# Trainium2 study: a closer-spaced SSD scan, earlier z loads, norm sums on VectorE and pooling weights split in the mixing stage of a hybrid decoder step

## The chip, the cores and the metric

One Trainium2 chip, one core. The kernel is one launch that computes the whole layer. The metric is device time in microseconds (us), the median of repeated executions. The profile is one further execution, taken with the hardware profiler. Engines: PE (TensorE matmul, with PEld for its weight loads), DVE (VectorE), ACT (ScalarE), POOL (GpSimd), SP (SyncE, which here issues nearly all transfers, from one queue in program order).

## What is computed

One layer on 1024 prompt tokens and 8 x 8 sample tokens, model width 1024, all in fp32. Cut to its frame:

```python
x = x + 0.5 * swiglu(rmsnorm(x, norm_ffn1), ffn1_w_in, ffn1_w_out)
mix = token_mixing(rmsnorm(x, norm_mix), ...)
x = x + mix
x = x + 0.5 * swiglu(rmsnorm(x, norm_ffn2), ffn2_w_in, ffn2_w_out)
# token_mixing:
u, z, xbc, dt_raw, gate_logits = split(hn @ w_in)
branch_pool = pool_mix(u_ext, ...) @ pool_w_out
xs, bm, cm = causal_conv(xbc)
y = ssd_scan(xs, dt, A, bm, cm, h0) + d_skip * xs
yg = y * silu(z)                       # then an RMS norm in 4 groups of 512 channels
branch_ssd = (norm(yg) * ssd_norm) @ ssd_w_out
mix = (gates[0] * branch_pool + gates[1] * branch_ssd) @ w_o
```

`ssd_scan` is the chunked Mamba-2 recurrence: chunks of 128 tokens, 32 heads in 4 groups. Each of the 8 sample sequences carries its own state of 32 x 64 x 128 numbers, which is read, updated and written back.

## The kernel before, in words

The tokens are held transposed (channels on partitions) in two halves: half 0 has 512 prompt tokens, half 1 has 512 prompt tokens and the 64 sample tokens (576 columns). Each fp32 product is made of three matmuls on split operands: high by high, low by high, high by low. Weights arrive as fp32 (`wraw`), ACT rounds them to a high part `wh` and DVE subtracts to get the low part `wl`. Weights that are used twice can be split once and kept in DRAM as two arrays ("parted"); `load_w` then loads the two parts, 512 KB in place of 256 KB, and no split is needed.

The stages, in order of time: FFN 1 (input product in a Winograd-like form, names `pw`; output product `po`), the mixing's input projection, the mixing itself, FFN 2. Beside FFN 1 a side chain, `part`, splits weights for later: it loads a block (`pr`), splits it, stores both parts (`part<-ph`, `part<-pr`), and goes on to the next. Before, it goes over 12 blocks of `ffn1_w_out`, 12 of `ffn2_w_in`, 16 of `w_o` and 16 of `pool_w_out`. At the end of the input product the kernel finishes what is left of it (`finish(side)`), before the hidden rows (`hr`, `hp`) are loaded for the output product.

The mixing stage runs, on PE: `pool_branch` for both halves (`pgm`, then `pbp` with `pool_w_out`), then for each half four products with `ssd_w_out` (`pso`, one for each group g of 512 channels; the fourth is inside `merge`), then `out_proj` with `w_o` (`pwo`). I call these the dense products. The input of the product of group g is the scan of that group: `ssd_group` goes over 4 chunks (5 in half 1, the fifth being the samples). Each chunk is a step `ssd_a` (load the decay rows `ab`, transposes `pxT`, products `pcb`, many DVE and ACT operations on `ab`), a state update `ssd_st` (`pst`, `hst`), and `ssd_b` (`pyo`, `pyd`). For samples `ssd_b` runs over 8 units, each of which loads 256 KB of state `h`, transposes it (`ph0T`), updates it on DVE (`pnew`, L1375) and stores it. After a group's last chunk `gating` multiplies the scan's output `xs` by `z`, sums squares (`sq`, `ssq`), sends the sum through PE (`pss`), takes the inverse root on POOL (`rsm`), scales, and splits the result into `yhl`, the input of `pso`.

What sets the order: scan, gating and side work are Python generators. Each yields a delay, counted in PE work issued so far (`pe[0]`); `tick()`, called between the dense products, steps the generator that is due first. `STEP` is the delay between the steps of a scan for each half, `STEP_S` that between the sample units, `GP` that in gating, `PART_PACE` that of the side chain. When a dense product needs a group that is not gated, `scanned()` steps the scan to its end at once, with nothing dense in between. A scheduler then lays out each engine's instructions and assigns buffers: 42 buffers `act` serve all these tiles, 3 hold `xs` of whole groups, and `gating` may be at most two groups ahead of the products (`freed`).

Of the kernel before, what the change touches and what calls it, by code (L numbers as in the profile page):

```python
# [12 lines left out]
ALU = mybir.AluOpType  # L13

P = 128
D = 1024
KD = D // P
# [13 lines left out]
NTOK = (512, 576)  # L31
# [9 lines left out]

PRODUCTS = (("1", 0), ("2", 1), ("6", 0), ("5", 2), ("7", 0), ("3", 2), ("4", 0))

STEP = (7.0, 7.0)
STEP_S = 2.5
POST = 1.0
GP = (0.7, 1.2)
HN_AT, HN_PACE = 25.0, 2.0
MP = 2.0
R_WAIT0 = 2.0  # L50
# [3 lines left out]
T_AT, T_PACE = 2.0, 1.5  # L54
TURN_AT, CONST_AT = 60.0, 40.0
HP, HP_ST = 40, 0
PART_AT, PART_W, PART_PACE = 20.0, 4.0, 2.5


@with_exitstack  # L60
def tile_hybrid_pool_ssd_macaron(
# [303 lines left out]

        tr(out, r[:n, i : i + 1].broadcast_to([n, P]), ident[:n, :n])

    def rstd(tiles, h, count, out, pace=1.0, E=None):

        N = NTOK[h]  # L370
        nch = 4 + h
        s = act((P, N), name="ssq")
        for i, x in enumerate(tiles):
            if i == 0:
                S.activation(s, x, AF.Square)
            else:
                q = act((P, N), name="sq")
                S.activation(q, x, AF.Square)
                (E or V).tensor_tensor(s, s, q, op=ALU.add)  # L379
            if i % 2:  # L380
                yield pace
        yield max(pace, 1.5)
        pt = psum("ps", "pss")
        for c in range(nch):
            n = P if c < 4 else NS
            mm(pt[:n, c : c + 1], s[:, c * P : c * P + n], ones[:, 0:1])
        sm = small((P, 3, 5), "rsm", 2, pool=sp)
        v = sm[:, 2, :nch]
        if h == 1:
            G.memset(sm[:, 2, 4:5], 1.0)  # L390
        V.tensor_scalar(sm[:, 2, :4], pt[:, :4], 1.0 / count, EPS, op0=ALU.mult, op1=ALU.add)
        if h == 1:
            V.tensor_scalar(sm[:NS, 2, 4:5], pt[:NS, 4:5], 1.0 / count, EPS, op0=ALU.mult, op1=ALU.add)
        rsqrt(sm[:, 0, :nch], v)
        yield R_WAIT0
        r = act((P, N), name="r")
        pr = psum("ps", "prb")
        for c in range(4):
            along(pr[:, c * P : (c + 1) * P], sm[:, 0], c)
        S.copy(r[:, :512], pr)  # L400
        if h == 1:
            along(pt[:, 64:128], sm[:, 0], 4, NS)
            S.copy(r[:, 512:], pt[:, 64:128])
        yield R_WAIT
        out.append(r)
        yield 1.5
# [791 lines left out]
    def side():  # L1198
        yield from part(ffn1_w_out[0], out01)
        yield from part(ffn2_w_in[0], [(kb, 4, c0 + ff * P) for ff in range(N_PLAIN[0]) for kb in (0, 4) for c0 in (0, FF)])  # L1200
        for w in (w_o[0], pool_w_out[0]):
            yield from part(w, [(kb, 4, m * P) for m in range(KD) for kb in (0, 4)])

    ffn(wi1, ffn1_w_out[0], prep1, after1, side=side())
    ahead_d = in_proj(prep1m)
# [7 lines left out]
    def reload(h):  # L1213
# [4 lines left out]
            t.append(x_)  # L1218
        return t

    def pool_branch(h):

        N = NTOK[h]
        fh, fl = [None] * KD, [None] * KD
        d = {k: v for k, v in enumerate(ahead_d)} if h == 0 else {}

        def fetch_d(gi):
            for k in (2 * gi, 2 * gi + 1):
                if k not in d:
                    d[k] = load_d(h, k)  # L1230

        fetch_d(0)
        for gi in range(4):
            if gi < 3:
                fetch_d(gi + 1)
            dh, dl = zip(*(d.pop(k) for k in (2 * gi, 2 * gi + 1)))
            for j, pg in enumerate(dense2(wg[gi], 0, 0, [(h, dh, dl)], ("ps", "ps"), name="pgm")):
                m = gi * 2 + j
                fh[m], fl[m] = act((P, N), F32R, "fh"), act((P, N), F32R, "fl")
                for pt, (a, b) in zip(pg[0], PIECES[h]):  # L1240
                    split(pt[:, : b - a], fh[m][:, a:b], fl[m][:, a:b], cols[:, i_ps + m : i_ps + m + 1])
        for m in range(KD):
            t = act((P, N), name="t0")
            dma(t, gd[h][m])
            pb = dense(pool_w_out[0], 0, KD, m * P, [(h, fh, fl)], name="pbp")[0]
            for pt, (a, b) in zip(pb, PIECES[h]):
                V.scalar_tensor_tensor(t[:, a:b], t[:, a:b], 1.0, pt[:, : b - a], op0=ALU.add, op1=ALU.mult)
            dma(accd[h][m], t)

    def sample_parts(g, Bf, xs4, dtd3):  # L1250


        out = []
        for i in range(2):
            tok = slice(512 + 32 * i, 544 + 32 * i)
            xr = act((P, 5, 96), name="xr")
            S.copy(xr[:, :4, :].rearrange("p j (r t) -> p j r t", r=3), xs4[:, :, tok].unsqueeze(2).broadcast_to([P, 4, 3, 32]))
            S.copy(xr[:, 4, :].rearrange("p (r t) -> p r t", r=3), Bf[:, tok].unsqueeze(1).broadcast_to([P, 3, 32]))
            px, pb = psum("ps", "px3"), psum("ps", "pb3")
            for j in range(4):  # L1260
                tr(px[:96, j * P : (j + 1) * P], xr[:, j, :], ident)
            tr(pb[:96, :P], xr[:, 4, :], ident)
            xd, X3 = act((P, 512), name="xd3")[:96], act((P, 512), F32R, "X3")[:96]
            V.tensor_tensor(xd.rearrange("p (h d) -> p h d", d=HD), px[:96, :].rearrange("p (h d) -> p h d", d=HD),
                            dtd3[:, i, g * HPG : (g + 1) * HPG].unsqueeze(2).broadcast_to([96, HPG, HD]), op=ALU.mult)
            S.activation(X3, xd, AF.Copy)
            V.tensor_tensor(X3[32:64], xd[32:64], X3[32:64].bitcast(F32), op=ALU.subtract)
            B3 = small((96, P), "B3", 1, F32R)
            S.activation(B3, pb[:96, :P], AF.Copy)
            V.tensor_tensor(B3[64:96], pb[64:96, :P], B3[64:96].bitcast(F32), op=ALU.subtract)  # L1270
            bb = act((P, 4, P), F32R, "bblk")[:96]
            V.tensor_tensor(bb, B3.bitcast(F32).unsqueeze(1).broadcast_to([96, 4, P]),
                            bsel3.unsqueeze(2).broadcast_to([96, 4, P]), op=ALU.mult)
            out.append((X3, bb))
        return out

    def ssd_a(h, g, c, Bf, Cf, xs4, dts):
# [11 lines left out]
        for q in range(nq):  # L1289
            ab = act((P, hq, L), name="ab")  # L1290
            if smp:
                dma(ab, acs_sd[g * HPG : (g + 1) * HPG].partition_broadcast(P))
            else:
                r0 = g * HPG + q * hq
                dma(ab, acs_d[h][c, r0 : r0 + hq].partition_broadcast(P))
            abs_.append(ab)
        yield
        px = psum("ps", "pxT")
        for j in range(4):
# [12 lines left out]
        V.tensor_tensor(xp[:L, :].rearrange("p (h d) -> p h d", d=HD), px[:L, :].rearrange("p (h d) -> p h d", d=HD),  # L1312
                        dt[:L, hcs].unsqueeze(2).broadcast_to([L, HPG, HD]), op=ALU.mult)
        if smp:
            xd = sample_parts(g, Bf, xs4, cdp[1])
        else:
            xd = act((P, 512), name="xd")
            V.tensor_tensor(xd[:L, :].rearrange("p (h d) -> p h d", d=HD), px[:L, :].rearrange("p (h d) -> p h d", d=HD),
                            dtd[:L, hcs].unsqueeze(2).broadcast_to([L, HPG, HD]), op=ALU.mult)
# [14 lines left out]
    def ssd_b(h, g, c, a, hold, Cf, y4, dts):  # L1334
# [8 lines left out]
        if smp:  # L1343
# [16 lines left out]
                S.copy(hT.rearrange("p b n -> p (b n)"), pt)  # L1360
                return hT

            h0s = {0: load(units[0]), 1: load(units[1])}
            hTs = {}
            yield STEP_S
            for i, (pr, bh) in enumerate(units):
                if i + 2 < len(units):
                    h0s[i + 2] = load(units[i + 2])
                hTs[pr], h0 = turn(h0s[i]), h0s.pop(i)
                yield STEP_S  # L1370
                gp = g * 4 + pr
# [58 lines left out]
        hstate[g] = hn_  # L1430
        return hold

    def ssd_group(h, g, Bf, Cf, xs4, dts):
        y4 = xs4
        prev = None
        step = STEP[h]
        for c in range(4 + h):
            ga = ssd_a(h, g, c, Bf, Cf, xs4, dts)
            next(ga)
            yield step  # L1440
            try:
                next(ga)
            except StopIteration as e:
                a = e.value
            yield step
            if prev:
                for w in ssd_b(h, g, *prev, Cf, y4, dts):
                    yield w
            prev = (c, a, ssd_st(h, g, c, a, dts))
# [9 lines left out]
            dma(new_ssm_p[0, 0, g * HPG : (g + 1) * HPG].rearrange("(q h) p n -> (h p) q n", h=2),  # L1459
                fo.rearrange("p (q n) -> p q n", n=P))  # L1460

    def gating(h, g, y4, out):

        N = NTOK[h]
        E = V if (h, g) == (1, NG - 1) else G
        zs = []
        for j in range(4):
            z = act((P, N), name="z")
            dma(z, zd[h][g * 4 + j])
            zs.append(z)  # L1470
            if j % 2:
                yield GP[0]
        for j in range(4):
            E.tensor_tensor(y4[:, j, :N], y4[:, j, :N], zs[j], op=ALU.mult)  # L1474
            if j % 2:
                yield GP[0]
        rr = []
        yield from rstd([y4[:, j, :N] for j in range(4)], h, 512, rr, GP[0], E)
        while h * NG + g - 2 >= freed[0]:
            yield 1.0  # L1480
        yh, yl = [], []
# [39 lines left out]
    def scan():  # L1521
# [4 lines left out]
        for i, (h, g) in enumerate(todo):  # L1526
            if (h, g) == (0, 1):
                dts.append(fetch_dts(1))
            nxt = fetch(*todo[i + 1]) if i + 1 < len(todo) else None
            yield from ssd_group(h, g, *cur, dts[h])  # L1530
            yn = []
            gated[h, g] = start(gating(h, g, cur[2], yn)), yn
            cur = nxt

    cs = start(scan())
# [205 lines left out]
```

## Time and profile before

| what | value |
|---|---|
| median of 3 runs | 3139.75 us (3139.26 to 3140.36) |
| profiled execution: its own time | 3142.46 us |
| profiled execution: span | 3140.7 us |
| DVE, ACT, POOL busy in the span | 1812.9, 1269.6, 1001.6 us |
| FFN 1 with its output product, about | 0 to 820 us |
| input projection, about | 820 to 1540 us |
| mixing (first `pgm` to last `pwo`) | 1543 to 2380 us |
| FFN 2 to the end | 2380 to 3140.7 us |

How to read it: the page's second part gives the busy tenths of each engine in 40 slices of 78.5 us. PE is the engine to look at first: where its digit is below 9, something else sets the pace. The row PEclk under it is the clock that was granted to TensorE, in tenths of full speed. A view of windows gives the same for any stretch of time: microseconds busy, then the count of instructions in brackets, for PE, PEld, DVE, ACT and POOL, then the granted clock, the share of the DMA engines' time, and GB/s. In the chain of waits each row is a start, a duration, and what the end of the program waited for then.

### The profile page before, as it was taken

The page shows a single profiled execution, that of the slowest core. Times are in us where ns is not written, and L with a number is a line of the kernel's source. Part 1 is how long each engine was busy: PE and PEld are TensorE (multiplying, and loading weights), DVE is VectorE, ACT ScalarE, POOL GpSimd, SP SyncE. Part 2 cuts the span into 40 slices and gives each one's busy share as a digit, 9 for nine tenths or more (in the row PEclk, how much of TensorE's full clock was granted, in tenths as well). Part 3 has the DMA queues.
Part 4 walks back from the last instruction along what each step waited for, and adds up shares of the span by engine and source line. Part 5 has one row for each costly group of instructions (what it writes and reads, how often), then busy time and mean ns, then how long its engine had stood idle before and what let it go on. Part 6 is the DMA issues. An engine that isn't in the chain of part 4 may idle for free.

```text
span 3140.7 us, 51060 instructions
## 1 busy us (share of the span) xinstructions
PE 2881.3 (92%) x18494; PEld 2615.7 (83%) x18494; DVE 1812.9 (58%) x3220; ACT 1269.6 (40%) x2592; POOL 1001.6 (32%) x1018
## 2 busy tenths in 40 slices
PE   7999996999999999999899879666789999999998
PEld 6999996789899999989788657654679999997898
DVE  6555556334654868778655667455776554444432
ACT  5454444222444545545433432323323444443322
POOL 6344443000323545555212232222123544441000
PEclk9999998999999999999999889777889999999999
DMA  4566557765433333333697769443466442226552
GB/s 135 169 218 203 181 174 237 229 195 166 113 110 108 95 118 126 94 123 101 224 305 250 227 197 293 138 126 117 143 232 199 151 132 83 83 73 222 180 179 77
DMA packets 526492, 512.17 MB, mean 163 GB/s; under 512 B 37140, under 2 KB 366728, under 8 KB 526232
## 3 DMA queue, kind: packets, MB, share of 16 engines
q1 hardware_dynamic: 526224, 508.91, 51.0%
q8 instruction: 145, 2.38, 0.3%
q14 instruction: 107, 0.88, 0.1%
q10 hardware_dynamic: 16, 0.00, 0.0%
HBM read 357.58 MB, written 151.44 MB: 162 GB/s over the span
## 4 chain that ended last, share of the span: by engine, by line
PE 66%; DVE 6%; DMA 5%; issue 3%; POOL 3%; ACT 2%; SPq 1%; POOLq 0%; ACTq 0%; DVEq 0%
PE pw L162 30%; PE po L162 17%; PE pso L162 5%; PE pbp L162 2%; PE pg L162 2%; PE pwo L162 2%; PE pu L162 1%; POOL xs L1474 1%; POOL ssq L379 1%; DMA h<-in_state_ssm_dram 1%; PE pyd L162 1%; PE pst L162 1%; DMA z<-zd 1%; DMA pr<-in_pool_w_out_dram 1%; DVE us L951 1%
## 5 line engine op out<-in xcount | busy, mean ns | idle before, releaser
L162 PE MATMUL pw<-X,wh 128*128 128x288 f32 (+1 forms) x2484 | 623.3, 330 | 13.0 <-ACT v L559 3.9
L162 PE MATMUL pw<-X,wl 128*128 128x288 f32 (+1 forms) x1644 | 472.7, 288 | 1.9 <-DVE wl L443 1.9
L162 PEld LDWEIGHTS pw<-X,wh 128*128 128x128 f32 x2484 | 418.0, 189 | 52.1 <-ACT v L559 4.8
L162 PE MATMUL pw<-hl,wh 128*128 128x512 f32 x1072 | 390.6, 399 | 4.6 <-DVE t L563 4.6
L443 DVE TENSOR_TENSOR wl<-s,wh 128x512 fp32r<-128x512 f32 x288 | 219.8, 764 | 199.8 <-ACT wh L442 180.3
L162 PE MATMUL pw<-hi,wh 128*128 128x288 f32 x1120 | 330.7, 295 | 0.2 <-DVE rb L1095 0.2
L162 PE MATMUL pw<-lo,wh 128*128 128x288 f32 x1120 | 329.7, 294 | 0.0
L162 PE MATMUL pw<-hi,wl 128*128 128x288 f32 x1120 | 329.7, 294 | 0.0
L162 PEld LDWEIGHTS pw<-X,wl 128*128 128x128 f32 x1644 | 310.7, 189 | 2.5 <-DVE wl L443 2.5
L436 POOL TENSOR_TENSOR s<-wraw,wraw 128x512 f32<-128x512 f32 x144 | 205.7, 1429 | 309.7 <-DVE wl L443 218.5
L294 DVE TENSOR_TENSOR wl<-wraw,wh 128x512 fp32r<-128x512 f32 x228 | 158.1, 695 | 251.9 <-ACT wh L293 240.3
L162 PE MATMUL pw<-hl,wl 128*128 128x256 f32 x1072 | 299.0, 279 | 1.1 <-DVE wl L443 1.1
L293 ACT ACTIVATE wh<-wraw 128x512 fp32r<-128x512 f32 x228 | 138.6, 609 | 363.7 <-PE po L162 234.3
L443 DVE TENSOR_TENSOR wl<-wraw,wh 128x512 fp32r<-128x512 f32 x216 | 166.2, 770 | 137.4 <-ACT wh L442 132.0
L162 PEld LDWEIGHTS pw<-hl,wh 128*128 128x128 f32 x1072 | 201.2, 188 | 42.0 <-DVE t L563 5.8
L162 PE MATMUL po<-hh,wh 128*128 128x288 f32 (+1 forms) x800 | 212.0, 325 | 25.5 <-ACT hh L354 25.3
L442 ACT ACTIVATE wh<-s 128x512 fp32r<-128x512 f32 x288 | 181.5, 630 | 130.9 <-PE pw L162 128.8
L162 PEld LDWEIGHTS pw<-hi,wh 128*128 128x128 f32 x1120 | 210.1, 188 | 12.2 <-DVE rb L1095 0.5
L162 PE MATMUL po<-hr,wh 128*128 128x288 f32 (+1 forms) x800 | 212.1, 324 | 0.0
L162 PE MATMUL po<-hh,wl 128*128 128x288 f32 (+1 forms) x800 | 211.9, 324 | 0.0
L162 PEld LDWEIGHTS pw<-lo,wh 128*128 128x128 f32 x1120 | 210.2, 188 | 0.0
L162 PEld LDWEIGHTS pw<-hi,wl 128*128 128x128 f32 x1120 | 210.1, 188 | 0.0
(384 smaller groups left out, 6345.7 us busy)
## 6 DMA issues: line engine op xcount, KB each, us to landing
wraw<-in_ffn_w_in_dram SPq DMA_DIRECT2D x188, 256.0 KB
wh<-part SPq DMA_DIRECT2D x156, 256.0 KB
wl<-part SPq DMA_DIRECT2D x156, 256.0 KB
wraw<-in_w_in_dram SPq DMA_DIRECT2D x144, 256.0 KB
wraw<-in_ffn_w_out_dram SPq DMA_DIRECT2D x120, 256.0 KB
part<-ph SPq DMA_DIRECT2D x64, 256.0 KB
part<-pr SPq DMA_DIRECT2D x64, 256.0 KB
ab<-acsd SPq DMA_DIRECT2D x64, 256.0 KB
```

What stands on the lines that cost most here:

```text
L162: T.matmul(out, lhsT, rhs, start=start, stop=stop, skip_group_check=free)
L293: S.activation(wh, raw, AF.Copy)
L294: V.tensor_tensor(wl, raw, wh.bitcast(F32), op=ALU.subtract)
L379: (E or V).tensor_tensor(s, s, q, op=ALU.add)
L436: G.tensor_tensor(t, a, b, op=op)
L442: S.activation(wh, a, AF.Copy)
L443: V.tensor_tensor(wl, a, wh.bitcast(F32), op=ALU.subtract)
L951: V.tensor_tensor(nx[:, 2 * sh - 1 : HIST + 512], cur[:, 2 * sh - 1 : HIST + 512], cur[:, sh - 1 : HIST + 512 - sh], op=ALU.add)
L1474: E.tensor_tensor(y4[:, j, :N], y4[:, j, :N], zs[j], op=ALU.mult)
```

## The change

Six things change:

1. The delay between scan steps goes from 7.0 to 5.0 (half 0) and 4.0 (half 1); that between sample units from 2.5 to 1.0; gating's first delay from 0.7 to 1.0.
2. The four `z` tiles of a group are loaded in `ssd_group`, with its fourth chunk, instead of at the start of `gating`.
3. In `gating`, the products `y * z` alternate between DVE and POOL (all were on POOL but for the last group), and the sums of squares are on DVE (they were on POOL but for the last group). The chain starts 1.2 after the scan's end.
4. `pool_w_out` leaves the side chain of FFN 1, whose pace goes from 2.5 to 3.0. `pool_branch` of half 0 loads it as `wraw`, splits it, and stores both parts (`keep=True`); half 1 loads the parts. Half 0 also loads the first two pairs of `d` tiles of half 1.
5. The sample tokens' copies `xr` are made in a step of their own (`spread`), before the delay that precedes the rest of that chunk.
6. Three sample states are loaded ahead instead of two.

```diff
-STEP = (7.0, 7.0)
-STEP_S = 2.5
+STEP = (5.0, 4.0)
+STEP_S = 1.0
 POST = 1.0
-GP = (0.7, 1.2)
+GP = (1.0, 1.2)
...
-PART_AT, PART_W, PART_PACE = 20.0, 4.0, 2.5
+PART_AT, PART_W, PART_PACE = 20.0, 4.0, 3.0
...
-                (E or V).tensor_tensor(s, s, q, op=ALU.add)
+                V.tensor_tensor(s, s, q, op=ALU.add)
...
-        for w in (w_o[0], pool_w_out[0]):
-            yield from part(w, [(kb, 4, m * P) for m in range(KD) for kb in (0, 4)])
+        yield from part(w_o[0], [(kb, 4, m * P) for m in range(KD) for kb in (0, 4)])
...
-            pb = dense(pool_w_out[0], 0, KD, m * P, [(h, fh, fl)], name="pbp")[0]
+            pb = dense(pool_w_out[0], 0, KD, m * P, [(h, fh, fl)], name="pbp", keep=True)[0]
...
+            if h == 0 and m in (4, 6):
+                early[1][m // 2 - 2] = load_d(1, m // 2 - 2)
...
+        if smp:
+            xrs = spread(Bf, xs4)
         yield
...
-            h0s = {0: load(units[0]), 1: load(units[1])}
+            h0s = {i: load(units[i]) for i in range(3)}
...
-                if i + 2 < len(units):
-                    h0s[i + 2] = load(units[i + 2])
+                if i + 3 < len(units):
+                    h0s[i + 3] = load(units[i + 3])
...
             next(ga)
+            if c == 3:
+                for j in range(4):
+                    z = act((P, NTOK[h]), name="z")
+                    dma(z, zd[h][g * 4 + j])
+                    zs.append(z)
             yield step
...
-        E = V if (h, g) == (1, NG - 1) else G
-        zs = []
         for j in range(4):
-            z = act((P, N), name="z")
-            dma(z, zd[h][g * 4 + j])
-            zs.append(z)
-            if j % 2:
-                yield GP[0]
-        for j in range(4):
-            E.tensor_tensor(y4[:, j, :N], y4[:, j, :N], zs[j], op=ALU.mult)
-            if j % 2:
-                yield GP[0]
+            (G if j % 2 and (h, g) != (1, NG - 1) else V).tensor_tensor(y4[:, j, :N], y4[:, j, :N], zs[j], op=ALU.mult)
+            yield GP[0]
         rr = []
-        yield from rstd([y4[:, j, :N] for j in range(4)], h, 512, rr, GP[0], E)
+        yield from rstd([y4[:, j, :N] for j in range(4)], h, 512, rr, GP[0])
...
-            gated[h, g] = start(gating(h, g, cur[2], yn)), yn
+            gated[h, g] = start(gating(h, g, cur[2], zs, yn), GP[1]), yn
```

How this moves instructions is seen at three places.

The first is SP's queue at the end of FFN 1's input product. `hd` are the hidden rows on their way out, `hr` and `hp` the same rows coming back for the output product, which takes `hd_0` first; `pr` and `part` belong to the side chain, `wh<-part` and `wl<-part` are the output product's weights. Before:

```order
L308 DMA pr_6417<-in_pool_w_out_dram 128x4x128
L677 DMA hr_6507<-hd_16_290 128x512
L283 DMA wh_6571<-part_1778 128x512
L283 DMA wl_6573<-part_1779 128x512
L314 DMA part_6422<-ph_6419 128x512
L315 DMA part_6423<-pr_6417 128x512
L308 DMA pr_6426<-in_pool_w_out_dram 128x4x128
L677 DMA hr_6512<-hd_17_291 128x512
L283 DMA wh_6587<-part_2382 128x512
L283 DMA wl_6589<-part_2383 128x512
L314 DMA part_6431<-ph_6428 128x512
L315 DMA part_6432<-pr_6426 128x512
```

With the change, at the same place:

```order
L574 DMA hd_21_295<-g_6046 128x512
L677 DMA hr_6291<-hd_0_274 128x512
L677 DMA hp_6335<-hd_10_284 128x512
L677 DMA hp_6339<-hd_11_285 128x512
L677 DMA hr_6358<-hd_15_289 128x512
L283 DMA wl_6429<-part_1795 128x512
L677 DMA hr_6296<-hd_1_275 128x512
L283 DMA wh_6411<-part_2332 128x512
L677 DMA hr_6363<-hd_16_290 128x512
```

The side chain's last rows are gone from here (its last block now stands before `hd_19`), and `hd_0` is read back right behind the last store of half 0, where before it stood behind five more blocks of the side chain.

The second is PE at the gating of group 1 of half 1: the scan's last rows (`pyT`, `pyd`, `pfin`), gating's `pss` and `prb`, and the next scan's first (`pxT`, `pcb`). Before:

```order
L166 MATMUL pyT_22412<-ident,yt_22410 128x128 x4
L162 MATMUL pyd_22418<-ab_22156,xdt_22167 64x64 x8
L166 MATMUL pfin_22429<-ident,hst_22153 128x128 x4
L162 MATMUL pss_22473<-ones,ssq_22462 128x1 x4
L162 MATMUL pss_22473<-ones,ssq_22462 64x1
L166 MATMUL prb_22485<-ident,rsm_22479 128x128 x4
L166 MATMUL pss_22473<-ident,rsm_22479 128x64
L166 MATMUL pxT_22559<-ident,xs_4082_21603 128x128 x4
```

With the change:

```order
L162 MATMUL pwo_22222<-mh_21335,wh_22223 128x512
L162 MATMUL pwo_22222<-ml_21336,wh_22223 128x512
L162 MATMUL pss_22001<-ones,ssq_21954 128x1 x4
L162 MATMUL pss_22001<-ones,ssq_21954 64x1
L166 MATMUL pxT_22012<-ident,xs_3902_20905 128x128 x4
L162 MATMUL pcb_22017<-bc_20904,bc_20903 128x128
L166 MATMUL pcb_22017<-ident,bc_20903 128x128
L166 MATMUL prb_22057<-ident,rsm_22007 128x128 x4
L166 MATMUL pss_22001<-ident,rsm_22007 128x64
L162 MATMUL pwo_22222<-mh_21335,wl_22225 128x512
L162 MATMUL pwo_22222<-mh_21404,wh_22223 128x512
```

Before, no dense product stands between the scan's end and `pss`, nor between `pss` and `prb`; with the change this gating stands inside half 0's `out_proj`, one projection earlier than its result is needed.

The third is SP's queue at the load of `z` for group 0 of half 1 before, and for group 2 of half 1 with the change (`fin` is the final state, stored at the end of a group's scan). Before:

```order
L1295 DMA ab_21610<-acsd_116 128x512
L1459 DMA out_dram<-fin_21598 128x4x128
L1295 DMA ab_21612<-acsd_116 128x512
L1469 DMA z_21614<-zd_0_184 128x576
L1469 DMA z_21616<-zd_1_185 128x576
```

With the change:

```order
L1304 DMA ab_22206<-acsd_116 128x512
L1304 DMA ab_22208<-acsd_116 128x512
L1454 DMA z_22210<-zd_8_192 128x576
L1454 DMA z_22212<-zd_9_193 128x576
L1454 DMA z_22214<-zd_10_194 128x576
L1454 DMA z_22216<-zd_11_195 128x576
L1606 DMA xspill_3_86<-x_4201_22073 128x512
```

`z` moved from behind the group's final state to the rows `ab` of its fourth chunk, ahead of the sample units.

More of the change, by code (lines that the diff above doesn't have):

```diff
@@ L366, in along, with rstd @@
         tr(out, r[:n, i : i + 1].broadcast_to([n, P]), ident[:n, :n])
-    def rstd(tiles, h, count, out, pace=1.0, E=None):
+    def rstd(tiles, h, count, out, pace=1.0):
         N = NTOK[h]
@@ L1219, in reload @@
         return t
+    early = {0: dict(enumerate(ahead_d)), 1: {}}
     def pool_branch(h):
@@ L1224, in pool_branch @@
         fh, fl = [None] * KD, [None] * KD
-        d = {k: v for k, v in enumerate(ahead_d)} if h == 0 else {}
+        d = early[h]
         def fetch_d(gi):
@@ L1248, in pool_branch, with spread @@
             dma(accd[h][m], t)
-    def sample_parts(g, Bf, xs4, dtd3):
+            if h == 0 and m in (4, 6):
+                early[1][m // 2 - 2] = load_d(1, m // 2 - 2)
+    def spread(Bf, xs4):
         out = []
@@ L1258, in sample_parts @@
             S.copy(xr[:, 4, :].rearrange("p (r t) -> p r t", r=3), Bf[:, tok].unsqueeze(1).broadcast_to([P, 3, 32]))
+            out.append(xr)
+        return out
+    def sample_parts(g, xrs, dtd3):
+        out = []
+        for i, xr in enumerate(xrs):
             px, pb = psum("ps", "px3"), psum("ps", "pb3")
@@ L1314, in ssd_a @@
         if smp:
-            xd = sample_parts(g, Bf, xs4, cdp[1])
+            xd = sample_parts(g, xrs, cdp[1])
         else:
@@ L1431, in ssd_st, with ssd_group @@
         return hold
-    def ssd_group(h, g, Bf, Cf, xs4, dts):
+    def ssd_group(h, g, Bf, Cf, xs4, dts, zs):
         y4 = xs4
@@ L1460, in ssd_group, with gating @@
                 fo.rearrange("p (q n) -> p q n", n=P))
-    def gating(h, g, y4, out):
+    def gating(h, g, y4, zs, out):
         N = NTOK[h]
-        E = V if (h, g) == (1, NG - 1) else G
-        zs = []
         for j in range(4):
-            z = act((P, N), name="z")
-            dma(z, zd[h][g * 4 + j])
-            zs.append(z)
-            if j % 2:
-                yield GP[0]
-        for j in range(4):
-            E.tensor_tensor(y4[:, j, :N], y4[:, j, :N], zs[j], op=ALU.mult)
-            if j % 2:
-                yield GP[0]
+            (G if j % 2 and (h, g) != (1, NG - 1) else V).tensor_tensor(y4[:, j, :N], y4[:, j, :N], zs[j], op=ALU.mult)
+            yield GP[0]
         rr = []
-        yield from rstd([y4[:, j, :N] for j in range(4)], h, 512, rr, GP[0], E)
+        yield from rstd([y4[:, j, :N] for j in range(4)], h, 512, rr, GP[0])
         while h * NG + g - 2 >= freed[0]:
@@ L1529, in scan @@
             nxt = fetch(*todo[i + 1]) if i + 1 < len(todo) else None
-            yield from ssd_group(h, g, *cur, dts[h])
-            yn = []
-            gated[h, g] = start(gating(h, g, cur[2], yn)), yn
+            yn, zs = [], []
+            yield from ssd_group(h, g, *cur, dts[h], zs)
+            gated[h, g] = start(gating(h, g, cur[2], zs, yn), GP[1]), yn
             cur = nxt
```

## The prediction

> **What bounds the kernel now.** I read the page's busy shares first, then the slices, which are the rows for PE and for its clock.
>
> ```profile
> span 3140.7 us, 51060 instructions
> PE 2881.3 (92%) x18494; PEld 2615.7 (83%) x18494; DVE 1812.9 (58%) x3220; ACT 1269.6 (40%) x2592; POOL 1001.6 (32%) x1018
> PE   7999996999999999999899879666789999999998
> PEclk9999998999999999999999889777889999999999
> ```
>
> PE bounds the kernel nearly everywhere: nothing moved from one engine to another helps where its digit is 9. Two places are open. One is a single 6 in the seventh slice, the end of FFN 1's input product. The other is the run from slice 23 to slice 30, the mixing stage, where the clock sinks too. Windows over the mixing:
>
> ```profile
> core 0: us, PE busy (x) PEld busy (x) DVE busy (x) ACT busy (x) POOL busy (x), PEclk, DMA share, GB/s
> 1543.00:1709.00 166.00, 154.02 (x980) 135.36 (x981) 86.95 (x193) 51.06 (x103) 29.35 (x25) 0.96 0.90 302
> 1709.00:1886.00 177.00, 137.67 (x673) 108.69 (x672) 117.51 (x232) 68.28 (x131) 51.94 (x44) 0.84 0.63 203
> 1886.00:1990.00 104.00, 80.43 (x472) 61.90 (x470) 60.31 (x136) 25.97 (x52) 25.44 (x20) 0.84 0.79 252
> 1990.00:2090.00 100.00, 67.80 (x490) 57.74 (x490) 53.42 (x132) 34.76 (x76) 22.50 (x19) 0.77 0.46 140
> 2090.00:2190.00 100.00, 68.27 (x486) 58.32 (x485) 58.51 (x148) 29.68 (x60) 22.46 (x19) 0.76 0.40 123
> 2190.00:2290.00 100.00, 70.65 (x504) 60.04 (x505) 66.07 (x161) 31.84 (x65) 14.45 (x13) 0.77 0.43 129
> 2290.00:2380.00 90.00, 84.59 (x589) 82.01 (x589) 63.45 (x93) 23.15 (x37) 27.82 (x23) 0.95 0.74 248
> ```
>
> Length less PE's busy time is its idle time: 12.0, 39.3, 23.6, 32.2, 31.7, 29.4 and 5.4 us. The five stretches from 1709 to 2290 hold 156 us of it. No other engine is near full there. So it is a latency, and the chain of waits, in the stretch of half 1's group 1, says which:
>
> ```profile
> 2074.20 5.39 DMA z<-zd
> 2079.73 1.39 POOL xs L1474
> ...
> 2087.99 1.41 POOL ssq L379
> 2089.44 2.18 PE pss L162 x10
> 2091.94 1.19 POOL rsm L362
> ...
> 2095.18 2.94 DVE xs L1484 x3
> ```
>
> The scan of this group has been run to its end alone, because the dense product wanted it; then `z` is fetched, multiplied and squared on POOL, summed, and for some 15 us PE has nothing. The price goes on after the pause (finer windows, same columns):
>
> ```profile
> 2074.00:2078.00 4.00, 0.00 (x0) 0.00 (x0) 0.00 (x0) 0.00 (x0) 0.00 (x0) 0.50 0.79 181
> 2090.00:2094.00 4.00, 2.43 (x13) 2.22 (x12) 0.22 (x2) 0.00 (x0) 1.18 (x1) 0.50 0.02 4
> 2094.00:2098.00 4.00, 3.46 (x14) 2.52 (x12) 2.82 (x3) 1.99 (x4) 1.23 (x2) 0.50 0.00 0
> 2098.00:2102.00 4.00, 3.23 (x14) 3.10 (x14) 3.95 (x8) 1.92 (x5) 0.00 (x0) 0.50 0.00 0
> 2102.00:2106.00 4.00, 4.00 (x26) 4.00 (x26) 1.78 (x4) 1.50 (x4) 0.00 (x0) 0.77 0.00 0
> ```
>
> Working again, PE has half its clock until about 2102: 9.1 us busy at 0.50 and 4.0 at 0.77, which at full clock would have taken 4.6 and 3.1. So each pause costs 5.5 us more than its length.
>
> **The end of FFN 1.** The side chain's last block on SP, and PE in the 60 us around this place and around the same place of FFN 2, whose side chain is long done by then:
>
> ```profile
> 541.90 0.45 SPq L308 DMA_DIRECT2D pr<-in_pool_w_out_dram  x1
> 500.00:560.00 60.00, 33.98 (x185) 28.03 (x184) 35.76 (x55) 29.00 (x55) 12.92 (x13) 0.80 0.81 269
> 2820.00:2880.00 60.00, 55.14 (x294) 46.18 (x293) 34.27 (x52) 25.61 (x49) 13.80 (x14) 0.97 0.71 236
> ```
>
> A block is loaded, split and stored before the next begins, and the rows `hr` wait behind it in SP's queue. In the new order the side chain ends two hidden rows earlier, even with its slower pace, and `hd_0` comes back at once. FFN 2 shows what is left: 55.14 - 33.98 = 21 us gained. Bounds: 15, if the slower chain leaves a little, and 24. **-21**.
>
> **The scan's spacing, the z loads, the xr step.** In the new order every group's gating stands among dense products, one to two products before its result is wanted. Both the idle time of the scan run alone and that of gating's chain should go, where it flows. What flowing costs is in three stretches of the same profile, where scan and dense products already alternate:
>
> ```profile
> 1572.00:1714.00 142.00, 135.25 (x908) 120.64 (x906) 81.56 (x182) 44.90 (x95) 33.15 (x28) 0.98 0.87 292
> 1725.00:1772.00 47.00, 47.00 (x253) 37.85 (x252) 37.05 (x78) 23.84 (x47) 4.41 (x4) 1.00 0.93 286
> 1876.00:1943.00 67.00, 64.50 (x330) 49.96 (x330) 57.87 (x114) 20.24 (x43) 18.03 (x13) 0.97 0.88 291
> ```
>
> Idle: 6.75 + 0 + 2.5 of 256 us, 3.6%, at a clock of 0.97 to 1.00, and in the last one with DVE busy 86%. Of the 425 us of PE work from 1709 to 2290 I leave 5% idle, 21 us, since seven gatings with two passes through PE are now inside it. 156 - 21: **-135**. Bounds: 90, if the gatings still cost 5 us and the chunks 1 us each, and 156. The third state loaded ahead and the earlier `xr` copies take their share of these waits, not more.
>
> **The clock.** I count six such pauses: two in 1709 to 1886, one in each of the next four. 6 x 5.5 = 33, of which I take **-30**; the low clock in the scans run alone, also visible in the stretches' 0.76 and 0.77, would be a bonus. Bounds 0 and 50.
>
> The Trainium skill, TensorE: Matmul & The Clock Gate, "What's actually happening", says that the clock is halved after an idle window of about 3.4 us and is whole again after about 3.4 us of sustained work. By this rule a pause costs 3.4 us at half speed, 1.7 us, six of them 10 us, and the forecast would be 20 us later. The trace agrees on the halving (0.50), not on the length: some 12 us, since the pieces of work after the pause have gaps and are not sustained. The measurement decides.
>
> **What the closer steps load onto others.** Moved to DVE: the sums of 7 groups (three each), 14 of the 28 products by `z`; new in the mixing: 16 splits of `pool_w_out`.
>
> ```profile
> L294 DVE TENSOR_TENSOR wl<-wraw,wh 128x512 fp32r<-128x512 f32 x38 | 26.5, 701 | 10.4 <-ACT wh L293 9.4 <-DMA wh<-part 1.0
> L379 DVE TENSOR_TENSOR ssq<-ssq,sq 128x576 f32<-128x576 f32 x9 | 7.7, 855 | 2.0 <-ACT sq L378 1.6
> L1474 DVE TENSOR_TENSOR xs<-xs,z 128x576 f32<-128x576 f32 x4 | 3.0, 758 | 4.1 <-DMA z<-zd 3.2 <-POOL xs L1410 0.9
> ```
>
> 16 x 0.701 + 21 x 0.855 + 14 x 0.758 = 40 us. DVE's busy time over the seven stretches is 506 us; 546 in the 672 that the two terms above leave of 837 is 81%, under the 86% that flowed. The transfers are 174 MB over the seven stretches (GB/s by length); with 4 MB more (next part) in 672 us that is 265 GB/s, under the 286 to 302 that flowed. Neither bounds the stage, but both are close, and what suffers is latency:
>
> ```profile
> ACT ea L1326 <- DMA ab<-acsd: 52.1, 13, 7.8
> ACT ea L1326 <- DMA ab<-acsd: 16.8, 4, 7.8
> 2029.87 5.52 DMA ab<-acsd
> ```
>
> (The waits from 1640 to 2350 and from 1572 to 1714: us in all, times, longest.) The rows `ab` take 5.5 us to come, and half 1's step is now 4.0. When they are late, ACT waits 52.1/13 = 4.0 us; queued behind it on ACT are the weights' `wh`, and on DVE, which waits for the same rows, `wl` and the emptying of PSUM. There are 36 chunks. Bounds: none late, 0; all late, 144. Four of the 13 fell into the first stretch that flowed, at a step of 7.0, and PE lost little by them; at the shorter steps I take ten more than now, each in full, **+40**.
>
> **Pooling weights.** Before, half 0 loaded 16 blocks as 512 KB of parts; now it loads 256 KB and stores 512 KB:
>
> ```profile
> pr<-in_pool_w_out_dram SPq DMA_DIRECT2D x16, 256.0 KB
> 1627.51 7.34 DMA d<-dl
> ```
>
> 16 x 256 KB more is 4.2 MB, 14 us at the 302 GB/s of the stretch 1543 to 1709, whose transfers are 90% busy. Its splits (11 us on DVE, as much on ACT) lie in a stretch where these engines are busy 87 and 51 of 166 us. I take half of the transfers, **+7**; bounds 0 and 14. The early `d` tiles remove the wait at 1627.51; PE still had work for most of it, **-2** (0 to 7).
>
> **Sum:** -21 - 135 - 30 + 40 + 7 - 2 = -141, and 3140.7 - 141 = 2999.7 for a profiled span. The profile before is 1 us above the median of its runs, so **2999 us**.
>
> **The rivals.**
>
> A. As summed, 2999; own range 2960 to 3040. Chance 0.66.
>
> B. All flows: no late `ab`, the whole bonus of the clock. -21 - 145 - 45 + 10 = -201, about 2940. For it: 1725 to 1772 has no idle at all. Against: seven gatings and 32 sample units now inside. 0.12.
>
> C. The wait for `ab` takes the place of the wait for gating: 28 of 36 late, 112 for 40, so 3071. For it: 5.52 against a step of 4.0. Against: a chunk's first DVE work is cheap to delay while dense products have weights. 0.13.
>
> D. Slower: SP's queue becomes the bound in half 1. A sample unit's store stands in SP's queue, waits for DVE's update, and the dense products' weights stand behind it, where before no dense product was near.
>
> ```profile
> 1950.98 4.92 DMA h<-in_state_ssm_dram
> ```
>
> If each of the 32 units starves PE for such a turn, 32 x 4.9 = 157 us are lost and the 141 are gone: 3155. It decides from 4.4 us per unit. Against: weights are loaded several blocks ahead, and a state's turn is shared by three in flight. 0.05.
>
> E. The mixing does not gain, since what is moved forward meets the same latencies in another place, and only FFN 1's 21 us come: 3119. 0.03; no change at all, 0.01.
>
> **How the numbers follow.** A measurement of this kernel can tell 0.2%, 6 us, from no change. Faster by more: A, B, C and E, 0.94; within: 0.01; slower: 0.05. The range has all of A, the nearer half of B and C's centre: 2945 to 3072.
>
> **What would show it.** Right: the seventh slice of PE at 8 or 9; `pss` waiting for `ssq` a few us in all; PEclk at 0.95 or more through the mixing; mixing about 120 us shorter, with DVE at some 80%. Wrong: `ab` or `h` at the head of the waits of PE, ACT and DVE in the mixing (C, D); a clock that stays low without pauses; idle time before `pbp` in half 0 above 20 us, which would make the +7 too small.

## The result and the profile after

The changed kernel takes 2984.89 us (median of 4 runs, 2982.28 to 2989.03) against 3139.64 for the kernel before: a ratio of 0.9508, 95% interval 0.9492 to 0.9525, 155 us less. The forecast was 2999. The profiled execution has a span of 2980.5 us.

The page after, its shares and the rows of its slices:

```profile
span 2980.5 us, 51010 instructions
PE 2842.1 (95%) x18494; PEld 2580.8 (87%) x18494; DVE 1838.0 (62%) x3255; ACT 1264.6 (42%) x2592; POOL 963.4 (32%) x983
PE   7999999999999999999988998798999999999998
PEclk9999999999999999999998999899999999999999
```

The single 6 in the seventh slice is a 9. The run of 6 to 8 of the mixing is shorter and shallower, with a 7 left in slice 26, and the clock no longer sinks below 0.8. The same 60 us at the end of FFN 1, and the mixing from its first `pgm` to its last `pwo` in eight stretches that end where a group's `pss` starts (columns as in the windows before):

```profile
500.00:560.00 60.00, 55.36 (x288) 45.91 (x287) 32.91 (x49) 25.31 (x49) 12.47 (x12) 1.00 0.78 259
```

```profile
1518.00:1609.00 91.00, 72.62 (x352) 54.37 (x350) 55.11 (x114) 34.93 (x68) 13.78 (x10) 0.89 0.88 289
1609.00:1672.00 63.00, 56.65 (x378) 49.88 (x377) 49.64 (x106) 27.75 (x59) 12.10 (x10) 0.92 0.88 297
1672.00:1778.00 106.00, 104.54 (x707) 90.20 (x706) 91.87 (x193) 48.40 (x99) 27.42 (x22) 1.00 0.82 266
1778.00:1855.00 77.00, 66.93 (x429) 49.54 (x429) 68.91 (x157) 34.70 (x70) 15.06 (x13) 0.96 0.84 260
1855.00:1957.00 102.00, 81.87 (x478) 60.87 (x478) 87.30 (x177) 36.56 (x73) 28.86 (x22) 0.90 0.76 241
1957.00:2035.00 78.00, 63.82 (x446) 51.14 (x447) 61.90 (x148) 32.10 (x68) 17.43 (x15) 0.91 0.72 231
2035.00:2104.00 69.00, 68.17 (x574) 63.06 (x574) 54.02 (x134) 28.11 (x61) 13.51 (x9) 0.96 0.62 188
2104.00:2219.00 115.00, 111.52 (x832) 110.09 (x831) 74.88 (x118) 24.77 (x40) 27.97 (x24) 1.00 0.75 253
1518.00:2219.00 701.00, 626.12 (x4184) 529.15 (x4182) 543.62 (x1144) 267.33 (x537) 156.13 (x125) 0.94 0.78 254
```

FFN 1's end: PE busy 55.36 of 60 us for 33.98, 21.4 us. The mixing: 701 us for 837, 136 less. Of these, 99 are idle time of PE (701 - 626.12 = 75 us for 174), and 37 are its busy time, 626 us for 663 with the same matmuls (4184 and 4186 recorded), at a mean clock of 0.94 for 0.85. The rest of the 155 to 160 us lies in the input projection, whose end came some 4 us earlier still, and in the scatter of the runs.

What PE waits for in the mixing now, longest first (us in all, times, longest):

```profile
PE pst L162 <- DVE xd L1329: 8.1, 5, 3.9
PE pso L162 <- DVE t L1589: 6.4, 3, 4.3
PE ph0T L166 <- DMA h<-in_state_ssm_dram: 6.0, 5, 2.0
```

Before, the head of this list was the long wait of the gating:

```profile
PE pss L162 <- POOL ssq L379: 67.3, 6, 16.9
```

Now `pss` waits for `ssq` 1.8 us in all. No single wait stands out; the 75 us left are many short ones, most of them in the first stretch (18 us, with transfers at 88%), in 1855 to 1957 (20 us, with DVE busy 87.30 of 102) and in the one after it (14 us).

### The profile page after: what moved, and what is told of

Same layout as the page of the kernel before. It is cut to its first block, busy times and chain, and to the rows that moved or that the text cites. A ratio compares the mean times of both kernels' runs of the same rounds, so it can differ in the third digit from the quotient of the medians.

```text
span 2980.5 us, 51010 instructions
## 1 busy us (share of the span) xinstructions
PE 2842.1 (95%) x18494; PEld 2580.8 (87%) x18494; DVE 1838.0 (62%) x3255; ACT 1264.6 (42%) x2592; POOL 963.4 (32%) x983
## 5 line engine op out<-in xcount | busy, mean ns | idle before, releaser
L294 DVE TENSOR_TENSOR wl<-wraw,wh 128x512 fp32r<-128x512 f32 x244 | 172.1, 707 | 253.4 <-ACT wh L293 247.5
L293 ACT ACTIVATE wh<-wraw 128x512 fp32r<-128x512 f32 x244 | 148.1, 609 | 365.7 <-PE po L162 239.2
L443 DVE TENSOR_TENSOR wl<-wraw,wh 128x512 fp32r<-128x512 f32 x216 | 163.9, 759 | 143.1 <-ACT wh L442 138.7
```

The source lines that it names most:

```text
L293: S.activation(wh, raw, AF.Copy)
L294: V.tensor_tensor(wl, raw, wh.bitcast(F32), op=ALU.subtract)
L443: V.tensor_tensor(wl, a, wh.bitcast(F32), op=ALU.subtract)
```

## Experiments

The spans of the mixing given below are read as above, from the first `pgm` to the last `pwo`. Times are medians; ratios are to the kernel before, with 95% intervals. "The changed kernel" has 0.9508 (0.9492 to 0.9525).

**The old delays, all else changed.**

```diff
-STEP = (5.0, 4.0)
-STEP_S = 1.0
+STEP = (7.0, 7.0)
+STEP_S = 2.5
```

> The changed kernel with the old delays (STEP 7.0 and 7.0, STEP_S 2.5) and all else as changed. If the spacing of the scan gives the gain of the mixing stage (my account): the late groups are again scanned alone, and it loses some 90 to 110 of the 136 us the mixing gained: 3075 to 3095 us. If the shorter gating chain (early z, sums on DVE) gives it: it loses at most 50, 3035 us or less.

3085.13 us, 0.9827 (0.9808 to 0.9846): 100 us are lost, as the account by spacing said. The mixing and the wait at the head of PE's list:

```profile
1516.00:2326.00 810.00, 667.33 (x4184) 564.08 (x4184) 546.05 (x1143) 272.87 (x539) 152.07 (x125) 0.86 0.68 220
PE pss L162 <- DVE ssq L379: 44.2, 8, 8.0
```

Most of the idle time (143 us, of 174 before), the low clock and most of the wait for the sum (44.2 us, of 67.3 before) are back, though `z` is early and DVE does the sums.

**The new delays, nothing else.** The reverse of the edit above, in the kernel before.

> The kernel before with the new delays alone (STEP 5.0 and 4.0, STEP_S 1.0). If the spacing gives the mixing's gain by itself: 136 less the 14 that gating's sums were seen to be worth and the few of z, so 3020 to 3040 us. If spacing works only together with the other edits (they are what lets it flow): 3070 us or more.

3041.04 us, 0.9689 (0.9665 to 0.9713), 97 us gained, 1 us outside of what was expected if the spacing suffices. The mixing takes 730 us, 107 of the 136. So the spacing does most of it without help, and the other edits add some 30 in the mixing. `pss` still waits there for the sums on POOL, 36.0 us in 7 waits.

**Gating on POOL, as before.** The products by `z` and the sums of squares of all groups but the last go back to POOL.

```diff
-                V.tensor_tensor(s, s, q, op=ALU.add)
+                (E or V).tensor_tensor(s, s, q, op=ALU.add)
...
-            (G if j % 2 and (h, g) != (1, NG - 1) else V).tensor_tensor(y4[:, j, :N], y4[:, j, :N], zs[j], op=ALU.mult)
+            E.tensor_tensor(y4[:, j, :N], y4[:, j, :N], zs[j], op=ALU.mult)
```

> The changed kernel with gating's products and sums on POOL, as before. By the spacing account gating's latency is hidden and DVE is relieved of 27 us: between 2975 and 2995 us. If the chain through POOL still holds PE at pss, some 3 us per group: 3005 or more.

2999.41 us, 0.9556 (0.9537 to 0.9576), 14 us slower than the changed kernel and between the two expectations. PE's longest wait in the mixing is again

```profile
PE pss L162 <- POOL ssq L379: 27.1, 6, 9.3
```

Spacing alone does not hide the chain through POOL: `pss` stands on PE at a place fixed by the count of PE work, and the chain is 4.5 us late there on average. Nor was DVE relieved by 27 us: its busy time in the mixing is 539.11 us for 543.62, although 35 operations left it, because its 288 operations `ab<-ab,dts` took 85.2 us where they take 65.6 in the changed kernel. Eight of them took 5.24 us at 1665.72, while POOL worked on gating, and 1.65 us at 1693.34, while it did not. So the 14 us may be the late chain, the slower DVE or both; this run does not separate them.

**z loaded in gating, as before.**

```diff
-            if c == 3:
-                for j in range(4):
-                    z = act((P, NTOK[h]), name="z")
-                    dma(z, zd[h][g * 4 + j])
-                    zs.append(z)
...
+        for j in range(4):
+            z = act((P, N), name="z")
+            dma(z, zd[h][g * 4 + j])
+            zs.append(z)
+            if j % 2:
+                yield GP[0]
```

> The changed kernel with z loaded at the start of gating, as before. If the spacing alone covers gating: the 5.4 us of a z load are hidden, since gating stands one or two products ahead: 2985 to 2995 us. If the early load is what removed the wait: up to 7 groups x 5.4 = 38 us, 3023.

2988.02 us, 0.9518 (0.9499 to 0.9537). The intervals overlap: with the new spacing the early load is worth 3 us or nothing.

**Two sample states ahead.**

```diff
-            h0s = {i: load(units[i]) for i in range(3)}
+            h0s = {0: load(units[0]), 1: load(units[1])}
...
-                if i + 3 < len(units):
-                    h0s[i + 3] = load(units[i + 3])
+                if i + 2 < len(units):
+                    h0s[i + 2] = load(units[i + 2])
```

> The changed kernel with two sample states loaded ahead instead of three. If state loads hold PE with the units 1.0 apart (32 units, a load some 4 to 5 us): 1 us per unit, 3015 us. If the queue has room for them: 2985 to 2992.

2988.01 us, 0.9528 (0.9508 to 0.9547): no difference that these runs can tell.

**Pooling weights in the side chain, as before, all else changed.** `pool_w_out` is back in `side`, `PART_PACE` is 2.5, and `pool_branch` has no `keep=True`.

> The changed kernel with the pooling weights back in the side chain of FFN 1 (old pace, no split in the mixing). FFN 1's end must lose its 21 us again; the mixing must gain what splitting there costs: 7 us by my account, so 2999 us in all. If the slow start of the mixing (26 us over what the same work takes later) comes from those splits and stores, it gains about 20 and the time stays at 2985.

2998.15 us, 0.9546 (0.9523 to 0.957), 13 us slower. The two places:

```profile
500.00:560.00 60.00, 32.72 (x189) 27.37 (x188) 35.13 (x54) 27.03 (x53) 13.59 (x14) 0.80 0.79 266
1548.00:2239.00 691.00, 623.32 (x4184) 527.90 (x4184) 534.44 (x1128) 258.31 (x523) 154.77 (x125) 0.95 0.76 251
```

FFN 1's end loses 22.6 us again, and the mixing takes 691 us for 701: splitting there costs 10.

**The pooling weights' move, nothing else.** The reverse of that edit, in the kernel before.

> The kernel before with the pooling weights out of FFN 1's side chain and split in the mixing, pace 3.0, and nothing else. FFN 1's end gains 21 us; the mixing, with its scan still spaced by 7.0, pays 7 by my sum and 8 by u_side: 3125 to 3127 us. If the splits are hidden at the old spacing: 3118.

3140.35 us, 0.9996 (0.9982 to 1.0009): no gain at all, outside both expectations. FFN 1's end did gain its 21 us, and the first `pgm` came at 1521.8 us for 1543.1; but the first `pso` came at 1709.6 for 1709.7. The two pooling branches took it all back. Where half 1's branch begins (windows, waits, and SP's rows):

```profile
1600.00:1640.00 40.00, 23.96 (x161) 21.27 (x160) 14.17 (x28) 9.46 (x21) 9.09 (x7) 0.79 0.89 303
PE pgm L162 <- ACT wh L293: 15.4, 1, 15.4
1598.53 0.46 SPq L290 DMA_DIRECT2D wraw<-in_pool_w_group_dram  x1
...
1619.96 2.00 SPq L290 DMA_DIRECT2D wraw<-in_pool_w_group_dram  x3
```

PE waits 15.4 us there for the weights of one pooling group, most of the 21 us that the move costs. SP issues the first of them at 1598.53, right behind half 0's stores of parts, and the other three only at 1619.96, behind half 1's first `d` tiles and a whole fetch of the scan. In the kernel before, these three stood ahead of the `d` tiles (at 1610.06, the tiles from 1612.05 on), so their place in the queue has moved. The transfers were busy 89% over these 40 us but only 21% from 1610.50 to 1614.50, so the load on them alone does not explain the wait. Why the order came out so, the runs do not show. The early `d` loads, which were not in this kernel, take some of these transfers out of that place; whether they, or the scan's other timing, make the difference to the 10 us above was not tried.

**The decay rows a chunk earlier**, in the changed kernel:

```diff
+        ahead_a = ssd_a(h, g, 0, Bf, Cf, xs4, dts)
+        next(ahead_a)
         for c in range(4 + h):
-            ga = ssd_a(h, g, c, Bf, Cf, xs4, dts)
-            next(ga)
+            ga = ahead_a
+            if c + 1 < 4 + h:
+                ahead_a = ssd_a(h, g, c + 1, Bf, Cf, xs4, dts)
+                next(ahead_a)
```

> The changed kernel with each chunk's decay rows ab loaded one chunk earlier. If late ab rows cost the 40 us that my sum gave them: 2945 to 2960 us. If they cost little (the waits are on ACT and DVE, and PE has other work): 2980 to 2990; above that, if the buffers they hold longer are missed elsewhere.

2981.14 us, 0.9497 (0.9481 to 0.9513). The wait, in the mixing of the changed kernel and then of this one:

```profile
ACT ea L1337 <- DMA ab<-acsd: 38.4, 17, 5.9
```

```profile
ACT ea L1337 <- DMA ab<-acsd: 9.5, 4, 5.0
```

The wait shrinks by 29 us and the kernel by 4, within the scatter; the mixing is 705 us, not shorter. ACT waits about as long as before, but for another operation, DVE's `cbm` (the changed kernel, then this one):

```profile
ACT btok L1321 <- DVE cbm L1317: 72.2, 24, 9.8
```

```profile
ACT btok L1321 <- DVE cbm L1317: 97.5, 29, 12.2
```

So loading the rows earlier is worth next to nothing. Whether the buffers that they hold longer cost part of a gain was not tried.

**Where DVE is full.** From 1855 to 1957 the merge of half 0 meets the scan and the gating of half 1:

```profile
1880.00:1900.00 20.00, 13.91 (x61) 10.25 (x61) 20.00 (x27) 5.00 (x10) 8.05 (x6) 0.73 0.60 203
1900.00:1920.00 20.00, 14.70 (x75) 10.52 (x74) 19.75 (x42) 6.53 (x15) 5.21 (x4) 0.91 0.76 255
```

DVE is busy 39.75 of these 40 us, and PE 28.6. Of PE's 20 us of idle time from 1855 to 1957, 14 are waits for DVE; the three longest:

```profile
PE pso L162 <- DVE t L1589: 4.3, 1, 4.3
PE pwo L162 <- DVE t L1589: 3.9, 1, 3.9
PE pso L162 <- DVE wl L294: 3.3, 3, 1.1
```

Two kernels test whether DVE sets the pace. One moves eight adds of that merge to POOL, the other gives DVE 24 more, whose results nobody uses:

```diff
-            V.tensor_tensor(t1[m], t1[m], acc[m], op=ALU.add)
+            (G if h == 0 else V).tensor_tensor(t1[m], t1[m], acc[m], op=ALU.add)
```

> The changed kernel with eight adds of half 0's merge (t1 + acc, 0.7 to 1.1 us each) on POOL instead of DVE. If DVE sets the pace of that stretch (it runs without a gap for 37 us there): 6 to 8 us gained, 2977 us. If it is the latency from one operation to the next that holds PE there: POOL's longer add (1.4 us) costs, 2985 to 2995.

2979.49 us, 0.9491 (0.9462 to 0.9519): 5 us less, the mixing 696 us; in the direction of the first account, not beyond the scatter.

```diff
+            if h == 0:
+                for _ in range(3):
+                    junk = act((P, N), name="junk")
+                    V.tensor_tensor(junk, acc[m], acc[m], op=ALU.add)
             V.tensor_tensor(t1[m], t1[m], acc[m], op=ALU.add)
```

> The changed kernel with 24 more DVE adds of 128x512 (some 0.8 us, 19 us in all, results unused) in half 0's merge. If DVE sets the pace there: 15 to 20 us longer, 3000 to 3005. If DVE has room there: 2985 to 2990.

2998.36 us, 0.9548 (0.9523 to 0.9573): 13 us longer, the mixing 714 us for 701, with 13 us more of DVE's busy time (556.41 for 543.62). What is added to DVE there comes out in the time, as it would if DVE set the pace of that stretch. It is not full proof: the added operations also stand in the merge's chain, ahead of the add whose result `pwo` takes, and so lengthen its latency. The first of the two kernels, with eight adds on POOL, lengthens that chain too but relieves DVE; it speaks for DVE's load, by 5 us that lie within the scatter.

**The splits beside the input projection**, in the changed kernel: a chain over the 16 blocks, started with the projection and finished at its end, and no `keep=True`.

```diff
+        pool_side = start(part(pool_w_out[0], [(kb, 4, m * P) for m in range(KD) for kb in (0, 4)]), 20.0)
...
-        for c_ in dts + [c]:
+        for c_ in dts + [c, pool_side]:
```

> The changed kernel with the 16 pooling blocks split beside the input projection, where transfers run at some 110 GB/s, neither in FFN 1 nor in the mixing. By u_side (3000 us span, of which 21 are FFN 1's end) the mixing gains some 8 us without the splits, and FFN 1's end stays short: 2975 to 2980 us. If the projection, with DVE busy three quarters, has no room: 2985 or more.

2978.8 us, 0.9489 (0.947 to 0.9509). The mixing takes 689 us for 701, as without the splits, but the projection ends 7 us later (first `pgm` at 1525.1 for 1517.7): 7 of the 12 us are paid there.

**Three of these together**: splits beside the projection, decay rows earlier, merge adds on POOL.

> The changed kernel with three edits together: pooling weights split beside the projection (alone 2979), decay rows loaded a chunk earlier (2981), half 0's merge adds on POOL (2979). If the three act at different places and add: 6 + 4 + 5 = 15 us gained, 2970. If they share one limit (transfers and DVE of the same stretches): no more than the best alone, 2976 to 2980.

2975.71 us, 0.9471 (0.9457 to 0.9484), the fastest of the runs, 9 us below the changed kernel, where the sum of the three would have been 15. The interval overlaps with that of the first edit alone (0.947 to 0.9509), so it is not shown that the other two add anything. The mixing:

```profile
1522.00:2207.00 685.00, 616.98 (x4184) 525.54 (x4184) 530.80 (x1119) 257.80 (x521) 169.90 (x133) 0.95 0.78 254
```

## Why the prediction came out as it did

The time was right within 14 us and inside case A's own range; most of its terms were right in kind, and four of them wrong in size. That it came so near is in part luck, as the third point shows.

- **What bounds the kernel.** Right. The latency of scans run alone and of their gating held PE; with the delays alone 97 of the 155 us come, and with the old delays 100 are lost again.
- **FFN 1's end, -21.** Measured 21.4, and 22.6 when undone. FFN 2's end was a true measure of it.
- **The scan's spacing, -135 of idle time, and the load on others, +40 for late `ab`.** Together -95. Idle time fell by 99, and by 106 in the run without the pooling splits (691 - 623.32 = 68 us for 174). But the two parts were wrong in ways that offset each other, and that is the luck. Over the mixing ACT waited for `ab` 17 times (38.4 us) where it had been 14 times (55.8), so the wait did not grow at the shorter steps, and removing 29 us of it moved nothing beyond the scatter. The +40 did not show: the row names a wait of ACT, not of PE. The idle time that I left, 21 us from 1709 to 2290 beside the 17 of the first and the last stretch, was too little: 75 are left. One reason shows, that I judged DVE by its mean over the stage (81%, measured 543.62 of 701, 78%), when it is the stretch that counts: 87.30 of 102 us where half 0's merge falls, and 39.75 of 40 in its middle, where 13 us of added DVE work lengthened the kernel by 13. What else is left, 18 us in the first stretch and 14 in the one after 1957 above all, was not traced to a cause.
- **The clock, -30.** Measured 37 us of busy time for the same matmuls. The mechanism was right; the bonus from the scans run alone, which I left out, may be part of the rest. The sign that I named, a clock of 0.95 or more through the mixing, came only in half of it: its mean is 0.94, and four of the eight stretches have 0.89 to 0.92. By the rule of the Trainium skill (TensorE: Matmul & The Clock Gate, "What's actually happening"), with 3.4 us at half speed after each pause, the estimate would have been 10. The trace agrees on the halving (0.50); the time back to full speed was longer here, some 12 us, perhaps because the work in it was not sustained, which no run tests.
- **Gating's sums and products on DVE.** I booked these as load alone, inside the DVE sum, and took the spacing to cover gating. They are worth 14 us: without them PE waits 27.1 us at `pss`, and DVE is spared only 4.5 us. The early `z`, which I counted within the spacing, is worth 3 or nothing, the third state the same.
- **Pooling weights, +7, and early `d`, -2.** Net 5; measured 10 in the changed kernel, and 21 alone in the kernel before. The sign that I named, idle time above 20 us before `pbp` in half 0, came close: the first stretch has 18. The early `d` tiles and the step for `xr` had no run of their own.
- **The rivals.** B, that all flows, was right that late `ab` cost little and wrong in the rest: 75 us of idle time are left, 20 of them where DVE is full, and its time was 45 us too low. C's wait is there in the profile (38.4 us), but earlier rows gained no more than the scatter. D and E did not come.

## What to carry to other kernels

Where an in-order engine idles for the latency of a chain that was started when its result was wanted, starting the chain earlier among independent work won back, here, most of the idle time and of the slow clock after it; shortening the chain's links was a second, smaller gain. Judge the relieved stage by its busiest stretch, not by its mean: the engine at 78% over the stage was at 99% where two phases came to overlap. And a wait of an engine off the critical path need not be a cost: the wait for `ab` fell by 29 us, and ACT waited for something else instead.

## What the runs showed of the hardware

After a pause of some 15 us PE's granted clock stayed at 0.50 through about 12 us of interrupted work (2090 to 2102 in the profile before). The same matmuls of the mixing (4184 recorded in each of these runs) took 667 us of busy time at a mean clock of 0.86 with the old delays, 626 at 0.94 in the changed kernel and 617 at 0.95 in the fastest one. With the 99 us of pauses that the change removed, 37 us of matmul time went too, so a pause cost here about 1.4 times its length on average. That is no fixed rate: in the changed kernel with the old delays there were 31 us less of pauses than in the kernel before (143 for 174), and no less matmul time (667 for 663).

DVE's operations could take longer beside POOL's. The 288 operations `ab<-ab,dts` of the mixing took 65.8 us in the kernel before and 65.6 in the changed kernel. They took 81.9 and 85.2 in the two kernels that have the close spacing and gating on POOL (the new delays alone, and gating on POOL), where gating runs beside the next scan. Why, these runs do not show.
